# YOCO decoder trunk on one core: output pages split earlier, prev multiplications and one diagonal tile given to VectorE, group 2 scaled in one step

## The chip, the cores and the metric

The kernel runs on one core of a Trainium2 chip, in one launch. The metric is the device time of one execution in microseconds (us). TensorE is called PE, VectorE DVE, ScalarE ACT, GpSimd POOL, and SyncE, which issues the DMAs here, SP.

## What is computed

A decoder trunk over 1024 tokens of width 1024, float32, with two layers. Layer A is gated linear attention. Layer B, which the change is about, is dilated sliding-window attention with eight heads; each head attends in three groups, with window and dilation (128, 1), (512, 4) and (2048, 16), and the three results are weighted by a softmax over their log-sum-exps:

```python
for gi, (window, dilation) in enumerate(SWA_GROUPS):
    o_g, lse_g = dilated_window_attention(q[:, :, gi], k_sh[:, :, gi], v_sh[:, :, gi], window, dilation)
    outs.append(o_g); lses.append(lse_g)
wts = jax.nn.softmax(jnp.stack(lses, axis=0), axis=0)
o = jnp.sum(wts[..., None] * jnp.stack(outs, axis=0), axis=0).reshape(bsz, s, SWA_OUT)
return (o.astype(x.dtype) * jax.nn.silu(g)) @ w_out
```

Keys and values have two heads, shared by four query heads each. Behind each layer stands `layer_norm(ALPHA * x + y)`.

## The kernel before, in words

**The scheduler.** The whole kernel is written as calls on an object `S` (class `Sched`), which records them as operations. `order()` then places them one by one with a table of assumed costs: it always takes the operation that can start first by these costs and, among those, the one with the smallest priority number, which is its place in the recording; `S.later(n)` shifts that number (a negative `n` is sooner). Only then `issue()` emits all of them from one line, L446, so every row of the profile carries L446 and operations are told apart by their tiles. An operation recorded on `S.vector`, `S.scalar` or `S.gpsimd` has its engine given; `S.va` leaves the choice of DVE or ACT to the scheduler, `S.vp` that of DVE or POOL, `S.vap` that of all three. A change of any cost, engine or number of operations thus moves others too.

**Large projections.** A product with a weight matrix is made of float32r passes with both operands split into a high and a low part: `mm3` issues wh·xh, wh·xl and wl·xh, each 128x512, into a PSUM tile `acc`. `split_hi` (ACT) and `split_lo` (`S.vp`) make the parts; weights come in as `wf` and become `wh` and `wl`. Pages of 128x1024 lie in the pools `p0` and `p1` (16 each). In layer B, `p1` holds the split input x1h and x1l, `p0` the rotation tables, K, V, Q, sg and og.

**Layer B by heads.** The work runs in eight units u = 0 to 7, one for each query head. `q_proj(u)` makes Q for three groups. `scores(u)` makes score tiles `lv` and from them the exponentials P (nine tiles of 128x512) and their statistics `sts`; these go through DRAM and come back in another order as `nat`, from which DVE makes the weights `ew`; those go through DRAM again (`cwd`) and come back as `cw` (L1362 to 1405). Group 2's columns cw[16:24] need no such trip: they are copied on the chip (L1395). `attend(u)` (L1407 on) does, in this order of recording:

- multiplies each block of P by its column of `cw`, groups 2, 1, 0 (L1433 to 1437); group 2 has eight blocks of 128x64, all in one tile;
- transposes group 2's tile into one PSUM tile `ms`, copies it in four quarters (64x256) to the two block-diagonal tiles `diag` (L1446 to 1450), multiplies by V into `po` (po<-diag), and copies that to the page `og`;
- calls `turn` (L1412) twice for group 1 and twice for group 0. Each call transposes four blocks into `ms` and makes two PT tiles: `prev` is a piece of P times the identity (one or two blocks at a time, L1427), `own` is the transposed block times a triangle (`upto`, DVE), and `copy_predicated` (DVE) puts the other triangle into `prev`; the PV matmuls po<-PT follow.

`g_proj(u)` is the projection for the gate, and `close(u)` multiplies it into og and, for u < 6, writes og to DRAM as `ogB[u]`. Units 0 to 3 run `g_proj` right after their scores. For units 4 to 7 all `g_proj` are recorded after `attend(6)`, then `attend(7)` and `close(7)` (L1517 to 1522); the scheduler uses their matmuls as filling between the small steps of attention.

**The end.** All eight og pages are needed in high and low parts (ogh, ogl) for the output projection `out_ln` (columns for the first half of the tokens, banks acc, lv and po) and `out_ln_rows` (second half, with the eight weight pages woh and wol). `load_og` reads a half page of `ogB` into a staging tile `ogf` and splits it. The staging tiles share the tag "a" of 13 tiles with P, diag and the rt tiles of the layer norm. The page loads are recorded after `layer_b` (L1548 to 1555), all into `p1`, where a page comes free when the last projection has read x1h or x1l; the wo pages go into `p0` (L1564).

Of the kernel before, what the change touches and what calls it, by code (L numbers as in the profile page):

```python
# [8 lines left out]
FR = mybir.dt.float32r  # L9
# [582 lines left out]
def trunk(tc, xT, wP, wA, wA12, wAv3, w2, wO, wK, wV0, wV12, wB, wOB, par_d,  # L592
# [13 lines left out]
    def split_hi(dst, src):  # L606
        S.scalar.activation(dst, src, AF.Copy)
# [437 lines left out]
    def small(name, tag, bufs, dt=F32, shape=(128, 512)):  # L1045
        return hp.tile(list(shape), dt, name=name, tag=tag, bufs=bufs)
# [118 lines left out]
            return ap.rearrange("p (n a e) -> p n a e", n=4, a=8)  # L1165
        return ap.rearrange("p (i r) -> p i r", r=DIL[g])

    def layer_b(xs):
        bmask = hp.tile([128, 256], F32, name="bmask", bufs=1)
        S.sync.dma_start(bmask, bmask_d)  # L1170
        rmask = hp.tile([128, 64], F32, name="rmask", bufs=1)
# [130 lines left out]
        def g_proj(u):  # L1302
            sg = page(p0, F32, "sg")
            U[u]["sg"] = sg

            def evac(half, acc):
                th = small("th", "t1", 2)
                S.scalar.activation(th, acc, AF.Tanh, scale=0.5)
                S.vector.scalar_tensor_tensor(sg[:, hs(half)], th, 1.0, acc, op0=OP.add, op1=OP.mult)
            project(wB[u, 3], xs, evac)  # L1310
# [96 lines left out]
        def attend(u):  # L1407
            P, cw, Vc = U[u]["P"], U[u]["cw"], V[u // 4]
            og = page(p0, F32, "og")
            U[u]["og"] = og  # L1410

            def turn(g, j0):  # L1412

                own, prev = (small("PT", "d", 4).rearrange("p (a b) -> p a b", a=4) for _ in range(2))
                pt = ps.tile([128, 4, 128], F32, name="ms", bufs=2)
                def has(x):
                    return x.rearrange("p (a two) b -> p a two b", two=2)[:, :, 1] if g else x[:, 0 if j0 else 1:]

                with S.group():
                    for i in range(4):  # L1420
                        p, o = P[g, j0 + i]
                        S.tensor.transpose(pt[:, i, :], blk(p[:, o:], BL[g][j0 + i][2] // 128 - 1), ident)

                for i in (0, 2):
                    front = pieces(P, g, j0 + i)[0]
                    n = front.shape[1]
                    S.vp.tensor_mul(prev[:, i + 2 - n:i + 2], front, ident[:, None, :].to_broadcast([128, n, 128]))  # L1427
                S.vector.tensor_mul(own, pt, upto.to_broadcast([128, 4, 128]))
                S.vector.copy_predicated(has(prev), below.to_broadcast(list(has(prev).shape)), has(pt))
                return own, prev  # L1430


            for g in (2, 1, 0):  # L1433
                for j in range(8):
                    p, o = P[g, j]
                    x = p[:, o:o + BL[g][j][2]]
                    S.vap.scale(x, x, cw[:, column(g, j):column(g, j) + 1])

            p = P[2, 0][0]
            pt = ps.tile([128, 4, 128], F32, name="ms", bufs=2)
            with S.group():
                for i in range(4):
                    S.tensor.transpose(pt[:, i, :], blk(p, i), ident)
            for k in range(2):  # L1446
                h = slice(k * 64, k * 64 + 64)
                for s in range(2):
                    S.va.copy(diag[s][h].rearrange("p (j k q) -> p j k q", j=4, k=2)[:, :, k, :],
                              pt[h, :, s * 64:s * 64 + 64])  # L1450
            po = [ps.tile([128, 512], F32, name="po", bufs=2) for _ in range(2)]
            with S.group():
                for s in range(2):
                    for j in range(4):
                        x = s * 4 + j
                        S.tensor.matmul(po[s][:, j * 128:j * 128 + 128], blk(Vc[2], x), blk(diag[s], j),
                                         start=True, stop=True)
            for s in range(2):
                for k in range(2):
                    x = s * 8 + k * 4  # L1460
                    S.vector.tensor_copy(
                        og.rearrange("p (n a e) -> p n a e", n=8, a=8)[:, :, :, x:x + 4],
                        po[s].rearrange("p (j k a n) -> p k n a j", j=4, k=2, a=8)[:, k])
            po = [ps.tile([128, 512], F32, name="po", bufs=2) for _ in range(2)]
            started = [False, False]

            def pv(bank, outv, vblk, rhs, last=False):
                S.tensor.matmul(outv, vblk, rhs, start=not started[bank], stop=last)
                started[bank] = True


            for r0 in (0, 2):
                own, prev = turn(1, 2 * r0)
                for r in (r0, r0 + 1):
                    i = 2 * (r - r0)
                    ov = [po[i].rearrange("p (i r) -> p r i", r=4)[:, r, :] for i in range(2)]
                    pv(0, ov[0], blk(Vc[1], 2 * r), own[:, i, :])
                    pv(1, ov[1], blk(Vc[1], 2 * r), prev[:, i + 1, :])
                    pv(1, ov[1], blk(Vc[1], 2 * r + 1), own[:, i + 1, :])

            for n0 in (0, 4):
                own, prev = turn(0, n0)
                for i in range(4):
                    n = n0 + i
                    out_n = po[n // 4][:, i * 128:i * 128 + 128]
                    if n:
                        pv(n // 4, out_n, blk(Vc[0], n - 1), prev[:, i, :])
                    pv(n // 4, out_n, blk(Vc[0], n), own[:, i, :], last=(i == 3))

            for i in range(2):  # L1490
                S.vector.tensor_add(og[:, hs(i)], po[i], og[:, hs(i)])
# [13 lines left out]
        for u in range(8):  # L1505
# [9 lines left out]
            if u == 3:  # L1515
                reload_kv()
        for u in (4, 5, 6, 7):  # L1517
            g_proj(u)
            if u < 7:
                close(u)  # L1520
# [22 lines left out]

    for half in range(2):
        out_ln(0, hs(half), lambda et: load_w(wO[et]), lambda et: xT[et * 128:et * 128 + 128, :], emit_a)
    U = layer_b(x1s)

    ogs.clear()  # L1548
    for kt in range(6):
        load_og(ogB[kt], kt, p1, lambda: small("ogf", "a", 13))  # L1550
    for u in (6, 7):
        hi, lo = og_page(u, p1)
        for half in range(2):
            split_hi(hi[:, hs(half)], U[u]["og"][:, hs(half)])
            split_lo(lo[:, hs(half)], U[u]["og"][:, hs(half)], hi[:, hs(half)])

# [4 lines left out]
    wo = []  # L1561
    for kt in range(NK):
        wf = wts.tile([128, 1024], F32, name="wf", bufs=2)
        hi, lo = page(p0, FR, "woh"), page(p0, FR, "wol")  # L1564
        with S.later(-EVAC):
            S.sync.dma_start(wf.rearrange("p (e c) -> p e c", e=NK), wOB[:, :, kt, :].rearrange("e p c -> p e c"))
            split_hi(hi, wf)
            split_lo(lo, wf, hi)
        wo.append((hi, lo))
# [96 lines left out]
```

## Time and profile before

| | us |
|---|---|
| median of 3 runs | 1158.88 |
| lowest and highest run | 1158.69, 1159.53 |
| the profiled execution's own time | 1158.02 |
| its span (first to last instruction) | 1156.2 |
| what lies around the span | 1.8 |
| PE busy / DVE / ACT / POOL | 1145.3 / 816.8 / 462.4 / 187.1 |

The mean granted clock of PE in it is 0.998. A row of the timeline gives the start in us from the span's begin, the duration, engine, line, operation, output tile<-input tiles, their sizes and types, and in brackets the engine's idle time before it with the instruction that ended it. Several like instructions in a row are drawn together (x4), and then the duration is from the first start to the last end. SPq rows are DMA issues, not the transfers. A row of grouped instructions gives count, busy us, mean ns of one, and idle time before them with the releasers.

### The profile page before, as it was taken

The numbers are of one execution on the slowest core, as the hardware profiler recorded it, in microseconds if no ns is written. First come the engines' busy times: TensorE is split into PE (matmuls) and PEld (weight loads), VectorE is DVE, ScalarE is ACT, GpSimd is POOL, SyncE is SP. The second block draws the span as 40 slices with busy tenths as digits, with TensorE's granted clock in tenths as the row PEclk, the third lists the DMA queues.
The fourth block names the chain that finished last, engine by engine and source line by source line (L and its number), as shares of the span: only waits on it lengthen the run. The fifth ranks groups of instructions, "written<-read, shape, count | busy, mean of one in ns | idle before, by whom it ended". The sixth has DMA issues, their size and how long they took to land.

```text
span 1156.2 us, 19776 instructions
## 1 busy us (share of the span) xinstructions
PE 1145.3 (99%) x7780; PEld 975.7 (84%) x7780; DVE 816.8 (71%) x1653; ACT 462.4 (40%) x970; POOL 187.1 (16%) x135
## 2 busy tenths in 40 slices
PE   9999999999999999999999999999999999999997
PEld 9888888889988888888888888888888878888886
DVE  6294952695977697765366768686778788768678
ACT  5355541555473344311215342434332434435242
POOL 1001000202222121321020303030211212103000
PEclk9999999999999999999999999999999999999999
DMA  8111122111144463643611111111141111124544
GB/s 270 55 39 37 65 83 87 42 57 55 57 170 124 150 206 137 193 142 104 209 44 33 55 38 56 38 52 42 38 165 38 20 39 38 39 75 146 190 140 180
DMA packets 93374, 108.40 MB, mean 94 GB/s; under 512 B 43648, under 2 KB 61952, under 8 KB 93280
## 3 DMA queue, kind: packets, MB, share of 16 engines
q1 hardware_dynamic: 93280, 107.13, 29.5%
q8 instruction: 61, 1.00, 0.4%
q14 instruction: 33, 0.27, 0.1%
HBM read 85.94 MB, written 21.17 MB: 93 GB/s over the span
## 4 chain that ended last, share of the span: by engine, by line
PE 96%; DVE 2%; DMA 1%; ACT 0%; issue 0%; POOL 0%; DVEq 0%; SPq 0%; POOLq 0%; ACTq 0%
PE acc L446 64%; PE lv L446 9%; PE po L446 9%; PE vac L446 8%; PE ms L446 4%; PE pro L446 2%; DVE t L446 0%; DMA xf<-in_xT 0%; DVE PT L446 0%; DMA wf<-in_wB 0%; POOL wl L446 0%; DVE P L446 0%; DVE rt L446 0%; ACT P L446 0%; DVE zz L446 0%
## 5 line engine op out<-in xcount | busy, mean ns | idle before, releaser
L446 PE MATMUL acc<-x1h,wh 128*128 128x512 f32 x608 | 250.9, 413 | 0.0
L446 PE MATMUL acc<-x1h,wl 128*128 128x512 f32 x608 | 237.5, 391 | 0.0
L446 PE MATMUL acc<-x1l,wh 128*128 128x512 f32 x608 | 236.9, 390 | 0.0
L446 ACT ACTIVATE wh<-wf 128x1024 fp32r<-128x1024 f32 (+2 forms) x104 | 108.1, 1041 | 288.2 <-PE acc L446 190.5
L446 POOL TENSOR_TENSOR wl<-wf,wh 128x1024 fp32r<-128x1024 f32 x39 | 93.5, 2396 | 634.6 <-ACT wh L446 450.9
L446 PEld LDWEIGHTS acc<-x1h,wl 128*128 128x128 f32 x608 | 114.1, 188 | 24.5
L446 ACT ACTIVATE P<-P,sts 128x128 f32<-128x128 f32 (+2 forms) x192 | 81.5, 425 | 129.0 <-DVE sts L446 128.5
L446 PEld LDWEIGHTS acc<-x1l,wh 128*128 128x128 f32 x608 | 114.5, 188 | 21.1
L446 PEld LDWEIGHTS acc<-x1h,wh 128*128 128x128 f32 x608 | 114.4, 188 | 20.9
L446 DVE TENSOR_TENSOR wl<-wf,wh 128x1024 fp32r<-128x1024 f32 (+2 forms) x66 | 83.7, 1268 | 61.3 <-ACT wh L446 48.4
L446 PE MATMUL acc<-xh,wh 128*128 128x512 f32 x256 | 102.4, 400 | 0.0
L446 PE MATMUL acc<-xh,wl 128*128 128x512 f32 x256 | 99.9, 390 | 0.0
L446 PE MATMUL acc<-xl,wh 128*128 128x512 f32 x256 | 99.8, 390 | 0.0
L446 DVE TENSOR_TENSOR t<-acc,cosT 128x512 f32<-128x512 f32 x60 | 41.4, 690 | 69.4 <-PE acc L446 68.8
L446 DVE TENSOR_TENSOR t<-acc,sinT 64x512 f32<-64x512 f32 x120 | 82.6, 688 | 1.6
L446 PE MATMUL lv<-K,Q 128*64 128x64 f32 (+2 forms) x512 | 69.2, 286 | 0.0
L446 DVE CUSTOM_DVE_ANT_0 P<-lv,bmask 128x256 f32<-128x256 f32 (+1 forms) x128 | 46.9, 379 | 23.3 <-PE lv L446 22.6
L446 DVE TENSOR_TENSOR Q<-t,t 128x512 f32<-128x512 f32 x45 | 62.2, 1383 | 1.3
L446 PEld LDWEIGHTS lv<-K,Q 128*128 128x128 f32 (+1 forms) x512 | 53.8, 163 | 9.6 <-issue 1.4
L446 PE MATMUL acc<-ogh,wh 128*128 128x512 f32 x152 | 59.9, 394 | 0.0
L446 PE MATMUL acc<-ogh,wl 128*128 128x512 f32 x152 | 59.2, 389 | 0.0
L446 PE MATMUL acc<-ogl,wh 128*128 128x512 f32 x152 | 59.2, 389 | 0.0
(251 smaller groups left out, 2228.2 us busy)
## 6 DMA issues: line engine op xcount, KB each, us to landing
wf<-in_wB SPq DMA_DIRECT2D x32, 512.0 KB
wf<-in_wA SPq DMA_DIRECT2D x24, 512.0 KB
wf<-in_wO SPq DMA_DIRECT2D x16, 512.0 KB
wf<-in_wOB SPq DMA_DIRECT2D x16, 512.0 KB
wf<-in_wV SPq DMA_DIRECT2D x12, 512.0 KB
res<-in_xT SPq DMA_DIRECT2D x16, 256.0 KB
x1d<-rt SPq DMA_DIRECT2D x16, 256.0 KB
out<-rt SPq DMA_DIRECT2D x16, 256.0 KB
```

Of the source, the lines that this page charges most:

```text
L446: getattr(handle[o.eng], meth)(*[conv(a) for a in args], **{k: conv(v) for k, v in kw.items()})
```

## The change

Five edits in layer B and at its end:

- A function `early()` is called before `g_proj(7)`. It loads and splits the og pages of units 0 to 3, first half and then second half, into `p0`, with priority 1000 places sooner. Pages 4 and 5 are loaded and 6 and 7 split as before into `p1`, now also half by half.
- The wo pages of kt < 4 go into `p1`, the other four into `p0`.
- The prev multiplications of `turn` go from `S.vp` to `S.vector`: all 64 run on DVE (before, 28 did and 36 ran on POOL, 25 of them 128x128 and 11 of them 128x256).
- The eight scales of group 2 in each unit (64 in all: 38 on DVE, 23 on ACT, 3 on POOL) become one DVE multiplication of 128x512 by the broadcast columns of `cw`.
- The four diag copies have fixed engines: DVE for the first tile, ACT for the second, 16 each in all (before, ACT had 23 and DVE 9).

```diff
--- before.py
+++ after.py
@@ -1165,7 +1165,7 @@
             return ap.rearrange("p (n a e) -> p n a e", n=4, a=8)
         return ap.rearrange("p (i r) -> p i r", r=DIL[g])
 
-    def layer_b(xs):
+    def layer_b(xs, early):
         bmask = hp.tile([128, 256], F32, name="bmask", bufs=1)
         S.sync.dma_start(bmask, bmask_d)
         rmask = hp.tile([128, 64], F32, name="rmask", bufs=1)
@@ -1424,13 +1424,16 @@
                 for i in (0, 2):
                     front = pieces(P, g, j0 + i)[0]
                     n = front.shape[1]
-                    S.vp.tensor_mul(prev[:, i + 2 - n:i + 2], front, ident[:, None, :].to_broadcast([128, n, 128]))
+                    S.vector.tensor_mul(prev[:, i + 2 - n:i + 2], front, ident[:, None, :].to_broadcast([128, n, 128]))
                 S.vector.tensor_mul(own, pt, upto.to_broadcast([128, 4, 128]))
                 S.vector.copy_predicated(has(prev), below.to_broadcast(list(has(prev).shape)), has(pt))
                 return own, prev
 
 
-            for g in (2, 1, 0):
+            x = P[2, 0][0].rearrange("p (j k q) -> p k j q", j=4, k=2)
+            w = cw[:, 16:24].rearrange("p (k j one) -> p k j one", k=2, j=4)
+            S.vector.tensor_mul(x, x, w.to_broadcast([128, 2, 4, 64]))
+            for g in (1, 0):
                 for j in range(8):
                     p, o = P[g, j]
                     x = p[:, o:o + BL[g][j][2]]
@@ -1446,8 +1449,8 @@
             for k in range(2):
                 h = slice(k * 64, k * 64 + 64)
                 for s in range(2):
-                    S.va.copy(diag[s][h].rearrange("p (j k q) -> p j k q", j=4, k=2)[:, :, k, :],
-                              pt[h, :, s * 64:s * 64 + 64])
+                    (S.scalar.copy if s else S.vector.tensor_copy)(
+                        diag[s][h].rearrange("p (j k q) -> p j k q", j=4, k=2)[:, :, k, :], pt[h, :, s * 64:s * 64 + 64])
             po = [ps.tile([128, 512], F32, name="po", bufs=2) for _ in range(2)]
             with S.group():
                 for s in range(2):
@@ -1515,6 +1518,8 @@
             if u == 3:
                 reload_kv()
         for u in (4, 5, 6, 7):
+            if u == 7:
+                early()
             g_proj(u)
             if u < 7:
                 close(u)
@@ -1543,14 +1548,20 @@
 
     for half in range(2):
         out_ln(0, hs(half), lambda et: load_w(wO[et]), lambda et: xT[et * 128:et * 128 + 128, :], emit_a)
-    U = layer_b(x1s)
-
-    ogs.clear()
-    for kt in range(6):
-        load_og(ogB[kt], kt, p1, lambda: small("ogf", "a", 13))
-    for u in (6, 7):
-        hi, lo = og_page(u, p1)
+
+    def early():
+        ogs.clear()
         for half in range(2):
+            for kt in range(4):
+                with S.later(-EVAC):
+                    load_og(ogB[kt], kt, p0, lambda: small("ogf", "a", 13), (half,))
+
+    U = layer_b(x1s, early)
+    for half in range(2):
+        for kt in range(4, 6):
+            load_og(ogB[kt], kt, p1, lambda: small("ogf", "a", 13), (half,))
+        for u in (6, 7):
+            hi, lo = og_page(u, p1)
             split_hi(hi[:, hs(half)], U[u]["og"][:, hs(half)])
             split_lo(lo[:, hs(half)], U[u]["og"][:, hs(half)], hi[:, hs(half)])
 
@@ -1561,7 +1572,8 @@
     wo = []
     for kt in range(NK):
         wf = wts.tile([128, 1024], F32, name="wf", bufs=2)
-        hi, lo = page(p0, FR, "woh"), page(p0, FR, "wol")
+        q = p1 if kt < 4 else p0
+        hi, lo = page(q, FR, "woh"), page(q, FR, "wol")
         with S.later(-EVAC):
             S.sync.dma_start(wf.rearrange("p (e c) -> p e c", e=NK), wOB[:, :, kt, :].rearrange("e p c -> p e c"))
             split_hi(hi, wf)
```

The recorded operations are placed anew. PE's order is the old one up to the first `attend`, and again from the start of `out_ln`; between them the same matmuls stand in another order. Three places follow. The names: acc<-x1h, wh is a pass of a g or q projection, ms<-ident,P are transposes, po<-diag and po<-PT are attention's products with V, lv<-K,Q are scores, and acc or lv<-ogh are passes of the output projection.

On PE, around unit 4's diagonal product, the order before has:

```order
L446 MATMUL ms<-ident,P 128x128 x4
L446 MATMUL acc<-x1h_4357,wh 128x512
L446 MATMUL acc<-x1l_4368,wh 128x512
L446 MATMUL acc<-x1h_4357,wl 128x512
L446 MATMUL acc<-x1h_4379,wh 128x512
L446 MATMUL acc<-x1l_4396,wh 128x512
L446 MATMUL acc<-x1h_4379,wl 128x512
L446 MATMUL po<-diag,V_7930 128x128 x8
```

The changed kernel has there:

```order
L446 MATMUL ms<-ident,P 128x128 x4
L446 MATMUL lv<-K_7875,Q 128x128
L446 MATMUL acc<-x1h_4240,wh 128x512
L446 MATMUL acc<-x1l_4248,wh 128x512
L446 MATMUL acc<-x1h_4240,wl 128x512
L446 MATMUL acc<-x1h_4250,wh 128x512
L446 MATMUL acc<-x1l_4264,wh 128x512
L446 MATMUL acc<-x1h_4250,wl 128x512
L446 MATMUL acc<-x1h_4279,wh 128x512
L446 MATMUL acc<-x1l_4289,wh 128x512
L446 MATMUL acc<-x1h_4279,wl 128x512
L446 MATMUL po<-diag,V_7900 128x128 x8
```

Nine passes of a projection and one score block stand between the transposes and the diagonal product where six passes stood.

On PE, at unit 6's turns (V_7923 and V_7894 are group 1's values, V_7918 and V_7885 group 0's), before:

```order
L446 MATMUL po<-PT,V_7923 128x128 x12
L446 MATMUL ms<-ident,P 128x128 x8
L446 MATMUL lv<-K_7905,Q 128x256
L446 MATMUL lv<-K_7905,Q 128x128
L446 MATMUL acc<-x1h_4357,wh 128x512
L446 MATMUL acc<-x1l_4368,wh 128x512
L446 MATMUL acc<-x1h_4357,wl 128x512
L446 MATMUL po<-PT,V_7918 128x128
```

And now:

```order
L446 MATMUL po<-PT,V_7894 128x128 x6
L446 MATMUL ms<-ident,P 128x128 x4
L446 MATMUL po<-PT,V_7894 128x128 x6
L446 MATMUL po<-PT,V_7885 128x128
L446 MATMUL ms<-ident,P 128x128 x4
L446 MATMUL po<-PT,V_7885 128x128 x6
L446 MATMUL acc<-x1h_4357,wh 128x512
L446 MATMUL acc<-x1l_4368,wh 128x512
L446 MATMUL acc<-x1h_4357,wl 128x512
L446 MATMUL po<-PT,V_7885 128x128 x8
```

Group 1's twelve blocks are parted by the first transposes of group 0, and six of them, without score or projection, stand between those transposes and group 0's first block.

On PE, at unit 7's last turns, before:

```order
L446 MATMUL po<-PT,V_7923 128x128 x12
L446 MATMUL ms<-ident,P 128x128 x4
L446 MATMUL po<-PT,V_7918 128x128
L446 MATMUL acc<-ogh_9878,wh 128x512
L446 MATMUL acc<-ogl_9926,wh 128x512
L446 MATMUL acc<-ogh_9878,wl 128x512
```

And now:

```order
L446 MATMUL po<-PT,V_7894 128x128 x12
L446 MATMUL ms<-ident,P 128x128 x8
L446 MATMUL acc<-ogh_9917,wh 128x512
L446 MATMUL acc<-ogl_9930,wh 128x512
L446 MATMUL acc<-ogh_9917,wl 128x512
L446 MATMUL lv<-ogh_9917,wh 128x512
L446 MATMUL lv<-ogl_9930,wh 128x512
L446 MATMUL lv<-ogh_9917,wl 128x512
L446 MATMUL po<-PT,V_7885 128x128
```

Both groups of transposes of group 0 come first, then six passes of the output projection, and then the first block. On SP, in front of that, before:

```order
L446 DMA cwd_9735<-ew 8x8x8 x4
L446 DMA wf<-in_wOB 128x1024
L446 DMA cw<-cwd_9735 128x8x1
L446 DMA cw<-cwd_9735 128x2x4
L446 DMA ogf<-ogB_6945 128x512 x2
```

And now:

```order
L446 DMA ogf<-ogB_6390 128x512
L446 DMA ogf<-ogB_6925 128x512
L446 DMA cwd_9741<-ew 8x8x8 x2
L446 DMA ogf<-ogB_7460 128x512
L446 DMA cwd_9741<-ew 8x8x8 x2
L446 DMA ogf<-ogB_7996 128x512
L446 DMA ogf<-ogB_9520 128x512
L446 DMA cw<-cwd_9741 128x8x1
L446 DMA cw<-cwd_9741 128x2x4
```

Five half-page loads stand among the transfers of unit 7's weights, where a single weight load (wf) stood.

## The prediction

> **What bounds the kernel now.** I read the page first: the busy time of each engine, then the engines in the chain that ended last.
>
> ```profile
> PE 1145.3 (99%) x7780; PEld 975.7 (84%) x7780; DVE 816.8 (71%) x1653; ACT 462.4 (40%) x970; POOL 187.1 (16%) x135
> PE 96%; DVE 2%; DMA 1%; ACT 0%; issue 0%; POOL 0%; DVEq 0%; SPq 0%; POOLq 0%; ACTq 0%
> ```
>
> TensorE is the bound. The change leaves the number of matmuls as it is, so all that it can give is TensorE time that passes without a matmul. The table of windows says where that is: compare each stretch's length with its "PE busy".
>
> ```profile
> core 0: us, PE busy (x) PEld busy (x) DVE busy (x) ACT busy (x) POOL busy (x), PEclk, DMA share, GB/s
> 0.00:600.00 600.00, 598.63 (x4736) 509.58 (x4737) 395.79 (x572) 248.75 (x348) 89.42 (x56) 1.00 0.34 112
> 600.00:890.00 290.00, 290.00 (x1622) 247.82 (x1621) 214.00 (x567) 106.76 (x346) 56.68 (x44) 1.00 0.20 54
> 890.00:950.00 60.00, 58.88 (x365) 49.40 (x364) 49.01 (x154) 23.09 (x82) 12.38 (x11) 1.00 0.15 37
> 950.00:1050.00 100.00, 100.00 (x570) 85.94 (x569) 76.04 (x235) 44.12 (x137) 15.31 (x14) 1.00 0.21 52
> 1050.00:1062.00 12.00, 11.18 (x84) 10.31 (x83) 10.61 (x21) 5.85 (x10) 9.66 (x8) 1.00 0.83 285
> 1062.00:1148.60 86.60, 86.60 (x412) 72.68 (x410) 67.46 (x101) 33.35 (x48) 3.69 (x2) 1.00 0.48 159
> 1148.60:1156.20 7.60, 0.02 (x1) 0.00 (x0) 3.85 (x7) 0.50 (x2) 0.00 (x0) 0.75 0.35 130
> ```
>
> The 1.37 us before 600 lie in layer A and the 7.58 us at the end behind the last matmul; the change reaches neither. Between them idle are 60 - 58.88 = 1.12 us in the stretch of units 4 and 5, and 12 - 11.18 = 0.82 us at the end of unit 7: 1.94 us. The timeline of TensorE in those stretches shows each wait in its brackets.
>
> ```profile
> 898.31 1.94 PE L446 MATMUL po<-diag,V 128*128 128x128 f32 x15 [0.34 <-DVE diag L446]
> 947.06 0.70 PE L446 MATMUL ms<-ident,P 128*128 128x128 f32 x4 [0.21 <-ACT P L446]
> 948.53 0.39 PE L446 MATMUL acc<-x1l,wh 128*128 128x512 f32 x1
> 948.75 0.40 PE L446 MATMUL acc<-x1h,wl 128*128 128x512 f32 x1
> 949.72 0.46 PE L446 MATMUL po<-diag,V 128*128 128x128 f32 x2 [0.57 <-DVE diag L446]
> ```
>
> 0.34 + 0.21 + 0.57 = 1.12. A wait costs slightly more than its bracket: a 128x512 matmul follows the last after 948.75 - 948.53 = 0.22 us, yet the row at 949.72 begins 0.97 us after the one at 948.75, so 0.75 are lost where the bracket shows 0.57. I take 0.17 more for each of the four waits. The ceiling on any gain is then 1.94 + 4 x 0.17 = 2.6 us, 0.22% of the median of 1158.88 us. A measurement of this kernel tells about 0.2%, 2.3 us, from no change.
>
> **Diag copies, one engine per tile.** The four copies out of one PSUM tile stand between group 2's transposes and po<-diag. Units 4 and 5 already give one tile to DVE and the other to ACT, so the trace shows what the fixed assignment does (unit 5, DVE and then ACT):
>
> ```profile
> 947.81 0.41 DVE L446 COPY diag<-ms 64x256 f32<-64x256 f32 x1
> 949.15 0.43 DVE L446 COPY diag<-ms 64x256 f32<-64x256 f32 x1 [0.92 <-ACT diag L446]
> 948.34 0.77 ACT L446 ACTIVATE diag<-ms 64x256 f32<-64x256 f32 x2
> ```
>
> They run in series: DVE until 948.22, ACT from 948.34 to 949.11, DVE from 949.15 to 949.58. DVE's second copy waits for ACT, with which it shares nothing but the PSUM tile, and the built order of the changed kernel holds the same waits between the engines. So no pair runs side by side: 1.77 us from first start to last end, where side by side would take about 0.85. That the change doesn't do what it says is thus part of the forecast here. The Trainium skill ("PSUM — Partial Sum Buffer", section "PSUM bank collisions raise a hardware error") makes two engines on one bank and quadrant at once an error, reads against reads included, which speaks against overlap here; by a reading with overlap unit 5 would give back about 0.7 us more.
>
> In the new order unit 4 has nine acc matmuls instead of six between its transposes and po<-diag. Three more are 3 x 0.22 = 0.66 us and cover its 0.34 wait: -0.34 - 0.17 = **-0.51**. Unit 5 keeps six and the same hand-overs, DVE, ACT, ACT, DVE: its 0.57 and its 0.21 stay. In units 0 to 3 the 290 us window is full and stays so.
>
> **Group 2's weights in one step.** Removed are eight 128x64 scales a unit, mostly on DVE; added is one DVE multiplication of two 512-wide SBUF inputs. Its nearest row is that of lnA, from DVE's groups after 600.
>
> ```profile
> 946.42 0.91 DVE L446 TENSOR_SCALAR P<-P,cw 128x64 f32<-128x64 f32 x5
> L446 DVE TENSOR_TENSOR lnA<-lnA,rt 128x512 f32<-128x512 f32 x6 | 4.2, 692 | 0.2
> ```
>
> In unit 5 it takes 0.69 for the 0.91 of five scales, beside which ACT did three. That is 0.2 us earlier at the ms transposes, at most the 0.21 that the row at 947.06 waited, or 0.2 later where more engines had shared the eight. The waiting matmul's latest input may be another, so I take **0**, with -0.38 to +0.2 as ends. In the other units a full window hides it; without that cover it costs the same 0.2.
>
> **Prev multiplications from DVE or POOL to DVE.** All 64 now go to DVE; 36 leave POOL.
>
> ```profile
> L446 DVE TENSOR_TENSOR PT<-P,ident 128x256 f32<-128x256 f32 x13 | 6.5, 515 | 0.0
> L446 DVE TENSOR_TENSOR PT<-P,ident 128x128 f32<-128x128 f32 x15 | 4.4, 312 | 8.2 <-issue 6.0 <-PE po L446 2.2
> L446 POOL TENSOR_TENSOR PT<-P,ident 128x128 f32<-128x128 f32 x25 | 15.6, 644 | 11.9 <-PE po L446 6.6 <-DVE P L446 2.9 <-ACT P L446 2.4
> L446 POOL TENSOR_TENSOR PT<-P,ident 128x256 f32<-128x256 f32 x11 | 9.3, 867 | 23.5 <-PE po L446 17.2 <-DVE sts L446 6.4
> ```
>
> That adds 25 x 0.312 + 11 x 0.515 = 13.5 us to DVE, which is busy for 76.04 of 100 us in the window of units 5 to 7, so it fits; each is also 0.33 to 0.35 us shorter. It matters only where TensorE reaches PV soon after its transposes. In units 4 to 6 the new order runs "PT x6, ms x4" before the first block of group 0, so six PV blocks, twelve passes, cover DVE's work instead of eight transposes and whole turns. The end of unit 7 prices both sides:
>
> ```profile
> 1054.73 1.95 PE L446 MATMUL po<-PT,V 128*128 128x128 f32 x16
> 1056.52 0.60 PE L446 MATMUL ms<-ident,P 128*128 128x128 f32 x4
> 1057.93 0.49 PE L446 MATMUL po<-PT,V 128*128 128x128 f32 x2 [0.82 <-DVE PT L446]
> 1055.15 2.13 DVE L446 TENSOR_TENSOR PT<-P,ident 128x128 f32<-128x128 f32 x2 [0.28 <-PE po L446]
> 1057.20 0.68 DVE L446 TENSOR_TENSOR PT<-ms,upto 128x512 f32<-128x512 f32 x1
> 1057.81 0.57 DVE L446 COPY_PREDICATED PT<-below,ms 128x384 f32<-128x384 uint8 x1
> 1053.19 5.22 POOL L446 TENSOR_TENSOR ogl<-ogf,ogh 128x512 fp32r<-128x512 f32 x4
> ```
>
> Sixteen passes take 1056.52 - 1054.73 = 1.79 us, so twelve take 1.34. Against them stand 0.68 of the upto product, with 0.57 of the predicated copy partly behind the first block, and ahead of them the two prev products, 0.31 + 0.52, which can begin before the transposes end. Upto and predicated alone (1.25) just fit; with half of the prev products late, about 0.42, the excess is 0.42 + 1.25 - 1.34 = 0.33 less slack of the same order as rounding. I take 0.25 a unit for units 4 to 6: **+0.75**, between 0 (prev done early) and 0.95 a unit (0.83 late, 1.25 behind it, less 1.34, and 0.17 each), so 0 to 2.8.
>
> **Pages split during the last gates.** In the rows above the wait of 0.82 comes from a DVE product of 128x128 that took most of 2.13 us for two, where 0.312 is its mean, while POOL made four ogl splits in 5.22. In the new order six og matmuls stand between unit 7's group-0 transposes and its first block of group 0: 6 x 0.22 = 1.3 us of work that no longer waits for attention. They cover the 0.82: **-0.82 - 0.17 = -0.99**. If the pages behind those matmuls were late, this gain would be gone and a wait stand in its place.
>
> What the splits are moved past: on SP the loads of pages 0 to 3 now stand between the transfers of unit 7's softmax weights (nat, cwd, cw), and on ACT the split of a page-4 half, loaded into the staging tile that group 2's transposes free, stands ahead of scales of P.
>
> ```profile
> 1046.25 4.79 SPq L446 DMA_DIRECT2D ogf<-ogB  x5
> 1055.25 0.63 ACT L446 ACTIVATE ogh<-ogf 128x512 fp32r<-128x512 f32 x1 [0.54 <-DMA ogf<-ogB]
> 1045.27 2.79 ACT L446 ACTIVATE P<-P,cw 128x256 f32<-128x256 f32 x7
> ```
>
> A load takes 4.79 / 5 = 0.96 to issue; the last of these five, issued by 1051.04, was there at 1055.25, 4.2 later, and its split took 0.63: 5.8 us from the transposes that free the tile. Until the transposes of groups 1 and 0, TensorE has 21 og matmuls and the sixteen passes of po<-diag: 21 x 0.22 + 1.79 = 6.4. In the 0.6 that are left two scales at 2.79 / 7 = 0.40 don't quite fit. I take **+0.3** with a hand-over, between 0 (no scale behind the split) and 0.6 (three). The wo pages only change places, and from the start of out_ln TensorE's order is the old one: nothing there.
>
> **The sum.** -0.51 + 0 + 0.75 - 0.99 + 0.3 = -0.45. On the profiled execution's 1158.02 us that is 1157.57; it lies 0.86 below the median of the runs, so against that median 1158.88 - 0.45 = 1158.4. With its bounds the forecast runs from 1158.88 - 0.51 - 0.38 - 0.99 = 1157.0 to 1158.88 - 0.51 + 0.2 + 2.8 - 0.99 + 0.6 = 1161.0.
>
> **Rivals.** *All waits go.* If the copies overlap after all, or the single multiplication brings unit 5's transposes forward enough, and units 4 to 6 cost nothing, the whole ceiling comes: 1158.88 - 2.6 = 1156.3. For it speaks that DVE's latest work in unit 5 does shrink; against it the serial copies in the rows at 947.81 to 949.58.
>
> *SP's queue (slower).* A page load takes a staging tile; with P and diag holding most of the 13, two are left, so every pair of loads waits until the pair before is split, and SP issues in order: nat, cwd and cw behind a waiting load wait with it. If cw comes one load landing later than the columns cover, 4.2 - 0.6 = 3.6 us stand in front of unit 7's transposes of groups 1 and 0: 1158.4 - 0.3 + 3.6 = 1161.7. It decides once cw lands more than those 0.6 us behind the page-4 split. For it: in the old order nearly all loads came after cw (the five at 1046.25 are the first long run of them). Against it: unit 7's scores end long before, with g_proj between.
>
> *Port.* DVE operations with two SBUF inputs have been held while POOL worked:
>
> ```profile
> 944.13 1.29 POOL L446 TENSOR_TENSOR Q<-t,t 128x512 f32<-128x512 f32 x1 [4.24 <-DVE t L446]
> 944.17 1.27 DVE L446 TENSOR_TENSOR zz<-ew,sts 128x8 f32<-128x8 f32 x1
> L446 DVE TENSOR_TENSOR zz<-ew,sts x8: 153/158/1271, 636.1 to 1035.8; 128x8 f32<-128x8 f32 x8
> ```
>
> A product of 0.158 (the median) took 1.27 and ended with POOL's. All 36 moved products become open to this: 1.27 - 0.16 = 1.1 lost each time one meets a POOL split of this length. The Trainium skill ("SBUF — State Buffer", section "SBUF: two separate sides") has such a DVE instruction and GpSimd's hold the shared ports exclusively, each for its whole length; the trace agrees, 1.27 us against 0.158. POOL is busy for only 15.31 of 100 us from 950 on, so of the about six products on a tight path one or two meet it: 1158.4 + 1.6 x 1.1 = 1160.2.
>
> **How the numbers follow.** Forecast 0.60 (its time lies within 0.2%), all waits go 0.13 (faster), port 0.10 (within 0.2%), SP's queue 0.17 (slower): faster 0.13, same 0.70, slower 0.17. The range takes in the first three, with the forecast's bounds: 1156.2 to 1161.0; left out is SP's queue, 0.17.
>
> **What would show it.** Right: busy TensorE from unit 4 to the end of unit 7 but for waits of some tenths; diag copies of unit 5 still one after another with its wait of about 0.6; no 0.82 in front of the first block of group 0 in unit 7; waits of 0.2 to 0.3 for PT in units 4 to 6. Wrong: a wait of over 1 us for P, cw or ogh in unit 7, an idle stretch in units 0 to 3, DVE products of over 1 us next to POOL's ahead of a waiting PV, or no wait at all from 890 to 1062.

## The result, and the profile after

| | before | after |
|---|---|---|
| median, us | 1158.28 (22 runs, 1157.61 to 1159.53) | 1160.36 (22 runs, 1157.97 to 1162.52) |
| profiled execution, us | 1158.02 | 1160.66 |
| its span, us | 1156.2 | 1158.9 |

The ratio after to before is 1.0017, with a 95% interval of 1.0011 to 1.0023. The changed kernel is slower by about 2 us, where 0.45 us faster was forecast. The time lies inside the range, and the change is smaller than the 0.2% named there, but its sign is the other one, and with 22 runs of each that is clear of the noise. The runs also spread over 4.6 us where those of before spread over 1.9.

First the busy times and the windows of the changed kernel, cut as before; the last matmul now starts 3.1 us later, so the end of the sixth window has moved.

```profile
PE 1146.7 (99%) x7780; PEld 976.2 (84%) x7780; DVE 821.7 (71%) x1662; ACT 452.0 (39%) x935; POOL 174.1 (15%) x105
core 0: us, PE busy (x) PEld busy (x) DVE busy (x) ACT busy (x) POOL busy (x), PEclk, DMA share, GB/s
...
600.00:890.00 290.00, 290.00 (x1621) 247.80 (x1620) 215.50 (x586) 101.82 (x326) 48.10 (x24) 1.00 0.20 54
890.00:950.00 60.00, 58.95 (x370) 49.88 (x369) 50.16 (x155) 19.88 (x74) 10.62 (x7) 1.00 0.16 37
950.00:1050.00 100.00, 99.53 (x563) 85.29 (x562) 75.08 (x216) 40.96 (x124) 12.38 (x9) 1.00 0.23 62
1050.00:1062.00 12.00, 11.91 (x73) 10.15 (x72) 11.26 (x26) 8.70 (x20) 4.47 (x3) 1.00 0.68 199
1062.00:1150.00 88.00, 85.92 (x416) 71.50 (x415) 68.59 (x101) 31.42 (x44) 9.23 (x7) 1.00 0.48 156
```

POOL is less busy (174.1 for 187.1 us) and DVE a little more, as the moved products say. TensorE's idle time has moved: 0.47 us from 950 to 1050, where there was none, and 2.08 us from 1062 to 1150, where there was none. Its timeline names the waits:

```profile
946.57 0.63 PE L446 MATMUL ms<-ident,P 128*128 128x128 f32 x4 [0.57 <-DVE sts L446]
...
949.05 1.13 PE L446 MATMUL po<-diag,V 128*128 128x128 f32 x8 [0.49 <-DVE diag L446]
...
997.91 2.02 PE L446 MATMUL po<-diag,V 128*128 128x128 f32 x16 [0.47 <-DVE diag L446]
...
1065.76 0.50 PE L446 MATMUL acc<-ogl,wh 128*128 128x512 f32 x1 [1.80 <-DVE ogl L446]
...
1128.46 0.50 PE L446 MATMUL ms<-sum,onesr 128*128 128x512 f32 x1 [0.23 <-DVE sum L446]
```

The waits of 0.34 (unit 4) and 0.82 (unit 7) are gone, but a new one of 1.80 us stands at the first low part of the og matmuls put in to cover the 0.82. What the other engines do ahead of it, first DVE, then POOL, then ACT:

```profile
1061.39 2.64 DVE L446 TENSOR_TENSOR PT<-P,ident 128x128 f32<-128x128 f32 x2
1063.95 2.35 DVE L446 TENSOR_TENSOR ogl<-ogf,ogh 128x512 fp32r<-128x512 f32 x2
```

```profile
1061.20 1.27 POOL L446 TENSOR_TENSOR ogl<-og,ogh 128x512 fp32r<-128x512 f32 x1 [5.86 <-ACT ogh L446]
1062.42 1.32 POOL L446 TENSOR_TENSOR ogl<-ogf,ogh 128x512 fp32r<-128x512 f32 x1
1063.71 1.44 POOL L446 TENSOR_TENSOR ogl<-og,ogh 128x512 fp32r<-128x512 f32 x1
```

```profile
1059.33 1.27 ACT L446 ACTIVATE ogh<-ogf 128x512 fp32r<-128x512 f32 x2 [2.68 <-DMA ogf<-ogB]
```

The high parts were there by 1060.6, so the load was not what came last. DVE's low parts stood behind two prev products that took 2.64 us. (A row that draws like instructions together gives the shape of the first; the second is 128x256, and the means are 0.312 and 0.515.) Then the low parts took 2.35 themselves. Nearly all of this, 1061.39 to 1066.30, lies beside three POOL splits in a row from 1061.20 to 1065.15. This is the forecast's rival "Port", but not at the products that it named: these two ran on DVE before the change as well (the 2.13 us row at 1055.15). The second theme is unit 6: DVE's second copy comes last of the four there, and TensorE waits for it.

```profile
996.08 0.42 DVE L446 COPY diag<-ms 64x256 f32<-64x256 f32 x1 [0.39 <-PE ms L446]
997.33 0.43 DVE L446 COPY diag<-ms 64x256 f32<-64x256 f32 x1 [0.83 <-ACT diag L446]
```

### The profile page after: what moved, and what is told of

It reads as the page before. It is cut to its first block, busy times and chain, and to the rows that moved or that the text cites. A ratio compares the mean times of both kernels' runs of the same rounds, so it can differ in the third digit from the quotient of the medians.

```text
span 1158.9 us, 19708 instructions
## 1 busy us (share of the span) xinstructions
PE 1146.7 (99%) x7780; PEld 976.2 (84%) x7780; DVE 821.7 (71%) x1662; ACT 452.0 (39%) x935; POOL 174.1 (15%) x105
## 4 chain that ended last, share of the span: by engine, by line
PE 92%; DVE 4%; DMA 2%; issue 1%; ACT 1%; DVEq 0%; ACTq 0%
PE acc L446 63%; PE po L446 8%; PE lv L446 8%; PE vac L446 8%; PE ms L446 4%; PE pro L446 2%; DMA wf<-in_wOB 2%; DVE rt L446 1%; DVE wol L446 0%; DVE PT L446 0%; ACT woh L446 0%; DVE t L446 0%; DVE P L446 0%; DVE ogl L446 0%; DVE sq L446 0%
## 5 line engine op out<-in xcount | busy, mean ns | idle before, releaser
L446 DVE TENSOR_TENSOR Q<-t,t 128x512 f32<-128x512 f32 x41 | 56.9, 1389 | 1.3
```

Of the source, the lines that this page charges most:

```text
L446: getattr(handle[o.eng], meth)(*[conv(a) for a in args], **{k: conv(v) for k, v in kw.items()})
```

## The experiments

Two theories came out of this. **Port**: in unit 7, DVE's operations on two SBUF tiles are held while POOL's splits run. **Order of the copies**: in units 5 and 6 the tile that po<-diag needs first is finished last. Rivals: the pages simply land late; the sum of four serial copies counts, not their order; DVE is overloaded; another edit is at fault. Five of the experiments keep a kernel's placed order, taken from `order()`, and alter only the operations named; the others undo a part and let the scheduler place anew. Each was timed beside the kernel before, which took 1158.49 us for the first eight and 1158.52 for the last two (1158.28 beside the changed kernel).

**1. The three splits on VectorE.** In the changed kernel's order:

```diff
-        done = self.order()
+        done = _placed(self.order())
+    last = [o for o in done if o.eng == "POOL" and o.writes and o.writes[0].buf.name[:3] == "ogl"]
+    for o in last[-5:-2]:
+        o.eng = "DVE"
```

> The changed kernel in its own order of instructions, but the three low-part splits that GpSimd makes at the end of unit 7 (two halves of page 6, one of page 5) are made by VectorE at their place in the order. Port theory: VectorE's two-input operations were held while GpSimd worked (2.64 us for two products, 2.35 for two splits), so the wait of 1.80 us for ogl goes, with about 0.18 of refill: 2.0 us less than the changed kernel, about 1158.4, and the spread of the runs shrinks. Rival, late pages: the loads land late whoever splits them, the wait stays and VectorE has 2 us more to do: no less than the changed kernel's 1160.4, up to 2 more. Rival, VectorE overloaded at that place: slower than the changed kernel.

Measured: 1158.49 us (1157.80 to 1160.06), 1.9 less than the changed kernel; ratio to before 1.0002 (0.9993 to 1.0011). DVE's operations at the same place:

```profile
1061.28 0.63 DVE L446 TENSOR_TENSOR PT<-P,ident 128x128 f32<-128x128 f32 x2
1061.83 1.29 DVE L446 TENSOR_TENSOR ogl<-ogf,ogh 128x512 fp32r<-128x512 f32 x2
```

0.63 and 1.29 us instead of 2.64 and 2.35, though DVE has three splits more to do, and the wait for ogl is gone. The pages were not late, and DVE was not overloaded. The profiled execution is the slowest of the eleven (1160.06): it waits 0.76 us in two places for weight pages of the output projection (wol), of which more below.

**2. Both copies of the first tile first.** In the changed kernel's order:

```diff
+    at = [i for i, o in enumerate(done) if o.calls[0][0] in ("copy", "tensor_copy") and o.writes[0].buf.name == "diag"]
+    for u in range(0, len(at), 4):
+        four = sorted((done[i] for i in at[u:u + 4]), key=lambda o: o.seq)
+        if u // 4 in (5, 6):
+            for i, k in zip(at[u:u + 4], (0, 2, 1, 3)):
+                done[i] = four[k]
```

> The changed kernel in its own order, but in units 5 and 6 both copies of the first diagonal tile (VectorE) come ahead of both of the second (ScalarE); the engines stay. Theory: the fixed engines finish the tile that TensorE needs first as the last of the four copies, and that makes the waits of 0.49 (unit 5) and 0.47 us (unit 6) before the diagonal product; both go, with 0.17 us of refill each: 1.3 us less, about 1159.1. Rival, it is the sum of four serial copies that counts, not their order: the waits move to the second tile's four blocks, and 0.4 us or less is gained. Rival, the gain is lost again at the end behind the late pages: the profile shows no wait in units 5 and 6, and the time stays at 1160.4.

Measured: 1159.47 us (1157.39 to 1161.44), 0.9 less than the changed kernel, which is not clear of the noise with runs that spread so far; ratio to before 1.0005 (0.9996 to 1.0014). The trace is clear. In unit 6, DVE, ACT and TensorE with this order:

```profile
995.10 0.86 DVE L446 COPY diag<-ms 64x256 f32<-64x256 f32 x2 [0.40 <-PE ms L446]
996.05 0.77 ACT L446 ACTIVATE diag<-ms 64x256 f32<-64x256 f32 x2 [0.91 <-DVE diag L446]
996.05 0.40 PE L446 MATMUL acc<-x1h,wl 128*128 128x512 f32 x1
996.29 1.39 PE L446 MATMUL po<-diag,V 128*128 128x128 f32 x11
```

No wait for diag in either unit, with four copies as serial as before: it is their order. Unit 7's po<-diag comes at 1051.70 instead of 1053.34, 1.64 earlier; 0.25 of that was there already at unit 5's transposes (946.32 for 946.57). Its wait for ogl, still 1.22 us, stays, and the profiled execution also waits 0.76 us for a weight page of the output projection, so not all of it arrives.

**3. Both together.** 

> The changed kernel's order with both mendings: the three low-part splits at the end of unit 7 on VectorE, and in units 5 and 6 both copies of the first diagonal tile first. If the two causes are separate, their gains add: 1160.4 - 1.9 - 1.3 = 1157.2, faster than before by about 1 us. If a load that lands late stands behind both (the pages of unit 7, or the weights of the output projection), what the copies give is lost there again: about 1158.5.

Measured: 1157.27 us (1156.90 to 1158.66); ratio to before 0.9990 (0.9981 to 1.0000). The gains add, as two separate causes would. The view of waits has two lines left, the first of them in layer A:

```profile
PE pro L446 <- DVE Dg L446: 1.2, 1, 1.2
PE ms L446 <- DVE sts L446: 0.6, 1, 0.6
```

**4. Splits on VectorE, and the same work put back on GpSimd for nobody.** On top of experiment 1; the mask tile bmask that it overwrites is no longer read at that point:

```diff
+    mask = next(v for o in done for v in o.reads if v.buf.name == "bmask").buf
+    again = View(mask, _np.broadcast_to(_np.arange(256).reshape(1, 256), (128, 256)))
+    for o in last[-5:-2]:
+        for half in (slice(0, 256), slice(256, 512)):
+            c = Op()
+            c.eng, c.func, c.first = "POOL", None, []
+            c.calls = [(m, (again, a[1][:, half], a[2][:, half]), kw) for m, a, kw in o.calls]
+            done.insert(done.index(o), c)
```

> The mended splits of unit 7 (three splits on VectorE) with three splits' work put back on GpSimd at the same place: it subtracts the same tiles in two halves each into the mask tile, which nobody reads any more, so nothing waits for it. Only GpSimd's presence beside VectorE differs. Port theory: VectorE's products and splits beside it are held again, products of 1 us and over in the trace, TensorE waits about 2 us for ogl or PT, 1160.4 or more. Rival, GpSimd's split was late as a producer and contention counts for nothing: the time stays at 1158.5 and the products at their 0.3 us.

Measured: 1159.76 us (1158.88 to 1160.87), 1.3 more than experiment 1; ratio to before 1.0013 (1.0004 to 1.0022). DVE and POOL at the place:

```profile
1061.12 0.84 DVE L446 TENSOR_TENSOR PT<-P,ident 128x128 f32<-128x128 f32 x2
1061.88 2.35 DVE L446 TENSOR_TENSOR ogl<-ogf,ogh 128x512 fp32r<-128x512 f32 x2
1064.15 0.68 DVE L446 TENSOR_TENSOR PT<-ms,upto 128x512 f32<-128x512 f32 x1
```

```profile
1060.74 1.81 POOL L446 TENSOR_TENSOR bmask<-og,ogh 128x256 f32<-128x256 f32 x2 [5.67 <-ACT ogh L446]
1062.63 2.21 POOL L446 TENSOR_TENSOR bmask<-ogf,ogh 128x256 f32<-128x256 f32 x2
```

Nothing waits for these POOL operations, and the two splits are back at 2.35 from 1.29. That shows contention without any dependence, and it costs TensorE a wait that experiment 1 does not have:

```profile
1069.06 1.16 PE L446 MATMUL po<-PT,V 128*128 128x128 f32 x8 [0.77 <-DVE PT L446]
```

The wait and the time are less than expected (about 2 us, 1160.4 or more): the two products ahead of the splits took 0.84, not far from the 0.63 of experiment 1, so less was held than in the changed kernel. It is the mechanism of the prediction's rival "Port". The Trainium skill ("SBUF — State Buffer", section "SBUF: two separate sides") puts it as an exclusive lock held for the whole instruction. The trace agrees: 1.06 us more for two splits, about one POOL operation of the row above (2.21 us for two).

**5. The early pages alone.** The kernel before with `early()` and the places of the wo pages, nothing else. Seen from the changed kernel, in extract:

```diff
-                    S.vector.tensor_mul(prev[:, i + 2 - n:i + 2], front, ...)
+                    S.vp.tensor_mul(prev[:, i + 2 - n:i + 2], front, ...)
...
-            S.vector.tensor_mul(x, x, w.to_broadcast([128, 2, 4, 64]))
-            for g in (1, 0):
+            for g in (2, 1, 0):
...
-                    (S.scalar.copy if s else S.vector.tensor_copy)(
+                    S.va.copy(
```

> The kernel before with only the early page splits (and the places of the wo pages); prev products, scales and diagonal copies are chosen by the scheduler as before. If the loss lies in the early pages at the end of unit 7: slower than before by 1 us or more, a wait for ogh or ogl in unit 7. If it lies in the edits of attend, or in the two together: the same as before or up to 1 us faster, since the wait of 0.82 us in unit 7 may go.

Measured: 1158.47 us (1157.44 to 1159.90); ratio to before 1.0001 (0.9992 to 1.0009). The early pages alone cost nothing and bring nothing that the runs tell; unit 7's wait for PT is 0.72 instead of 0.82.

**6. The edits of attend alone.** The changed kernel with the page loads, `p0` and `p1` of before, in extract:

```diff
-    U = layer_b(x1s, early)
+    U = layer_b(x1s)
...
-            if u == 7:
-                early()
```

> The changed kernel without the early splits: prev products on VectorE, one multiplication for group 2, and fixed engines for the diagonal copies. If the loss lies in the early pages: within 0.6 us of before (unit 4's 0.51 gained, up to 0.9 lost by the order of the copies in units 5 and 6), about 1158.5. If it lies in attend: slower than before by 1 us or more.

Measured: 1166.38 us (1165.87 to 1167.14); ratio to before 1.0067 (1.0054 to 1.0081). The loss was expected here if it lay in attend (1 us or more), but not of this size. Unit 7's weights come late: cw is issued at 1046.45 where before issued it at 1040.80 (SP's rows; before first).

```profile
1040.80 1.00 SPq L446 DMA_DIRECT2D cw<-cwd  x2
```

```profile
1046.45 1.00 SPq L446 DMA_DIRECT2D cw<-cwd  x2
```

The scales and the prev products then fall on POOL's splits. TensorE, DVE (for the scales the tile's view, with shortest, median and longest in ns), and POOL:

```profile
1060.74 1.22 PE L446 MATMUL po<-PT,V 128*128 128x128 f32 x4 [3.54 <-DVE PT L446]
```

```profile
L446 DVE TENSOR_SCALAR P<-P,cw x8: 340/850/1462, 1050.8 to 1056.9; 128x256 f32<-128x256 f32 x7, 128x128 f32<-128x128 f32 x1
```

```profile
1057.20 1.41 DVE L446 COPY og<-po 128x256 f32<-128x256 f32 x4
1058.53 1.55 DVE L446 TENSOR_TENSOR PT<-P,ident 128x128 f32<-128x128 f32 x2
1060.00 0.68 DVE L446 TENSOR_TENSOR PT<-ms,upto 128x512 f32<-128x512 f32 x1
1060.60 0.43 DVE L446 COPY_PREDICATED PT<-below,ms 128x256 f32<-128x256 uint8 x1
```

```profile
1049.83 2.37 POOL L446 TENSOR_TENSOR wl<-wf,wh 128x1024 fp32r<-128x1024 f32 x1 [3.84 <-ACT wh L446]
1052.46 2.54 POOL L446 TENSOR_TENSOR ogl<-ogf,ogh 128x512 fp32r<-128x512 f32 x2 [0.26 <-ACT ogh L446]
1055.58 1.29 POOL L446 TENSOR_TENSOR ogl<-ogf,ogh 128x512 fp32r<-128x512 f32 x1 [0.57 <-ACT ogh L446]
1058.56 5.22 POOL L446 TENSOR_TENSOR ogl<-ogf,ogh 128x512 fp32r<-128x512 f32 x4 [1.70 <-ACT ogh L446]
```

A scale takes 0.34 us at its shortest and up to 1.46 here. Unit 7's waits are 0.24, 0.36, 0.84 and 3.54 us, 4.2 more than the 0.82 of before. Of the rest of the 8, the most is TensorE's clock: from the long wait on it was granted at half for some microseconds (windows as above; the clock is the third number from the end).

```profile
1060.00:1062.00 2.00, 1.26 (x5) 1.27 (x6) 2.00 (x5) 0.84 (x2) 2.00 (x2) 0.50 0.68 219
1062.00:1066.00 4.00, 4.00 (x17) 3.71 (x17) 2.23 (x5) 2.49 (x5) 2.74 (x3) 0.50 0.25 88
1066.00:1068.00 2.00, 2.00 (x16) 1.87 (x15) 1.25 (x3) 0.00 (x0) 0.39 (x1) 0.96 0.00 0
```

From 1060.74 to 1066 half of 5.3 us is lost, some 2.6 us by estimate. In the changed kernel cw is issued later still, yet no scale is waited for; 21 og matmuls of the early pages now stand on TensorE between group 2's transposes and those of groups 1 and 0:

```profile
1050.53 1.00 SPq L446 DMA_DIRECT2D cw<-cwd  x2
```

So with attend edited as it is, the early pages save 6 us. What moved DVE's weight chain back was not tried apart.

**7. The kernel before, with both copies of the first tile first, in units 4 and 5.** The edit of experiment 2 with `(4, 5)`, in the order of before.

> The kernel before in its own order, but in units 4 and 5 both copies of the first diagonal tile come ahead of both of the second, engines as they are. If it is the order of the copies that makes TensorE wait, the 0.34 of unit 4 and the 0.57 of unit 5 go, with 0.17 of refill each: 1.25 us less than before, about 1157.2. If the four serial copies count as a whole: the same as before.

Measured: 1157.07 us (1156.70 to 1159.24); ratio to before 0.9991 (0.9982 to 1.0000), 1.4 us less in the medians. In unit 5, DVE, ACT and TensorE:

```profile
947.68 0.85 DVE L446 COPY diag<-ms 64x256 f32<-64x256 f32 x2
```

```profile
948.63 0.77 ACT L446 ACTIVATE diag<-ms 64x256 f32<-64x256 f32 x2 [0.42 <-DVE diag L446]
```

```profile
948.86 1.39 PE L446 MATMUL po<-diag,V 128*128 128x128 f32 x11
```

The first tile is ready at 948.53; TensorE starts at 948.86 without a wait, while ACT still copies the second. This is, with experiment 3, the fastest kernel of the study.

**8. Without the prev edit.** The first hunk of experiment 5's diff, in the changed kernel.

> The changed kernel with the prev products left to the scheduler's choice of VectorE or GpSimd, as before. If moving them to VectorE is what lays the tight products beside GpSimd's splits, the 1.8 us wait in unit 7 goes and the time is about 1158.5. If the wait belongs to the early pages and their splits alone, it stays: about 1160.4. GpSimd's products of 0.64 to 0.87 us on the path of PT may cost up to 1 us by themselves.

Measured: 1158.08 us (1156.34 to 1159.59); ratio to before 0.9998 (0.9989 to 1.0007). The wait for ogl is gone. The products beside POOL's splits are still slow:

```profile
1058.40 2.33 DVE L446 TENSOR_TENSOR PT<-P,ident 128x128 f32<-128x128 f32 x2 [0.55 <-PE po L446]
```

But in this order no split that TensorE needs next is queued behind them. Unit 6's wait for diag is gone as well: its copies now run DVE, ACT, DVE, ACT, and the first tile is finished by the third. So of the edits this one, on top of the others, decides whether these two waits stand, by the order that follows from it and not by the products' own time.

**9 and 10. Without the fixed engines; without the one multiplication.** The third and the second hunk of experiment 5's diff, each by itself in the changed kernel.

> The changed kernel with the diagonal copies' engines left to the scheduler. It still puts units 5 and 6 in the order VectorE first tile, ScalarE, ScalarE, VectorE first tile, and the end of unit 7 is the changed kernel's but for the copies. If the fixed engines are not the cause of either wait, both stay (0.5 us in units 5 and 6, 1.8 in unit 7): about 1160.4. If they are: about 1159.1 or less.

Measured: 1160.00 us (1158.92 to 1161.61); ratio to before 1.0013 (1.0004 to 1.0022). The waits of 0.48 and 0.47 in units 5 and 6 are unchanged; in unit 7, 0.90 for ogl and 0.87 for PT make the same sum as the 1.80. The fixed engines are not the cause: left free, the scheduler puts the copies of units 5 and 6 in the same order.

> The changed kernel with eight scales of group 2 in place of the one multiplication. The end of unit 7 has the same order on TensorE and GpSimd as the changed kernel, so by the port theory the wait for ogl stays there, near 1.8 us. In units 5 and 6 the second copy of the first diagonal tile now comes third of four instead of last: its waits should shrink by about 0.4 us each. Together 1159.6. If the one multiplication is what makes unit 7 late, the wait for ogl goes and the time is 1158 or less.

Measured: 1160.25 us (1158.83 to 1162.38); ratio to before 1.0016 (1.0007 to 1.0025). The wait for ogl is there with 1.78 us, as the port theory has it. The waits for diag did not shrink as expected: 0.40, 0.39 and 0.49 in units 4, 5 and 6. I had misread that order: only unit 5 has the first tile's second copy third, and its wait is 0.39 instead of 0.49; units 4 and 6 have it last. Unit 4 has six passes again ahead of its diagonal product, so its wait is back, and unit 5 has its three passes again ahead of its transposes, whose wait of 0.57 is gone.

## Why the prediction was wrong

Counted from the brackets of the two profiled executions, with the prediction's 0.17 for each wait that comes or goes (an estimate):

| step | forecast | measured |
|---|---|---|
| unit 4's po<-diag | -0.51 | -0.51 |
| unit 5's po<-diag | 0 | -0.08 |
| unit 5's transposes | 0 (-0.38 to +0.2) | +0.36 |
| unit 6's po<-diag | not in the sum | +0.64 |
| PT in units 4 to 6 | +0.75 | 0 |
| unit 7: the 0.82 before PT | -0.99 | -0.99, and +0.26 at group 1's first block |
| unit 7: pages ahead of their matmuls | +0.3 | +1.97 |
| output projection | 0 | +0.40 |
| sum | -0.45 | +2.05 |

The two profiled executions differ by 2.64 us. Of the 0.6 left over, 0.4 was there before anything changed on TensorE: unit 0's first transposes start at 653.17 instead of 652.78, and up to there its order is the old one. The last matmul starts 3.08 us later (1151.42 for 1148.34), so another 0.6 behind that point is not traced; the part after the last matmul is 0.4 shorter.

**The step that failed**, the largest of several, is "Pages split during the last gates": that the six og matmuls were "work that no longer waits for attention". They do not wait for attention's data, but their low parts are made on DVE, in DVE's queue behind attention's prev products, and beside POOL. The sentence "if the pages behind those matmuls were late, this gain would be gone and a wait stand in its place" is what happened, only that no load was late: experiments 1 and 4 show that POOL's neighbouring splits made DVE late, 1.97 us where the sum had +0.3. The sign that I had listed as wrong, DVE products of over 1 us next to POOL's, is in the trace. The rival "Port" had the mechanism and nearly the time (1160.2), with a chance of 0.10. The time is in part luck: it priced moved products, while the held ones had been on DVE before; it lacked the 0.64 and 0.36 of units 6 and 5, and it had a +0.75 that did not come. I had seen the hold in the very row that I used for the gain (2.13 us for two products beside 5.22 us of POOL; I read both as 128x128, but the second, of 128x256, took 1.50) and credited its removal without asking where POOL's next splits would fall.

**Diag copies.** That they stay serial held in every trace. (The two halves lie on different partitions, 0 to 63 and 64 to 127, so the rule on bank and quadrant that the prediction leaned on bears on two copies of the same half alone. Why the others are serial as well was not tested.) But I priced only their sum. Unit 5 was taken as evidence that the hand-overs do not change, and unit 6 was not looked at: before, its first tile was finished by the third copy, on ACT at 997.25, and TensorE came just then; now it is finished by the last. Before, ACT and TensorE:

```profile
996.87 0.38 ACT L446 ACTIVATE diag<-ms 64x256 f32<-64x256 f32 x1 [0.48 <-DVE diag L446]
997.31 0.94 PE L446 MATMUL po<-diag,V 128*128 128x128 f32 x6
```

Experiments 2 and 7 show the order at work, in both kernels.

**PT in units 4 to 6.** The +0.75 was not there: no wait for PT before unit 7. That is the end of the range that I gave as 0, with the prev products done early.

**Unit 5's transposes** wait 0.36 longer because TensorE is there sooner: in the new order three passes fewer stand between the scores and the transposes. That group 2's multiplication itself, 0.69 us, is no loss was right.

**Unit 4** came out as worked out. **SP's queue** did not decide: cw came 10 us later, and the matmuls of the early pages covered it; the 0.09 at group 1's first block is all that can be left of the +0.3.

**Output projection.** The waits of 0.2 to 0.8 us for sum and wol appear in the changed kernel and in experiments 1, 2, 4, 7 and 8, and not in 3, 5, 6, 9 and 10 or in the profile before. Experiment 7, which loads its pages as before, has one of 0.22. The weight pages follow one another through two buffers. ACT's idle time for their loads from 1070 on differs between the profiled executions, but the waits do not follow it: 16.8 us before, 17.7 in the changed kernel, 23.4 in experiment 2, and 22.1 in experiment 3, where TensorE never waited. Whether the change adds to it stays open.

## What to carry to other kernels

Before crediting a gain to work that is moved beside a tight spot, look at which engine makes its operands and what runs beside that engine there: here a VectorE operation on SBUF tiles next to a GpSimd one took up to its own time plus most of a GpSimd operation's (a scale of 0.34 us took 1.41 beside a split of 1.27). Where several serial steps feed one consumer, finish first what the consumer takes first; reordering two copies took away waits of 0.34 to 0.57 us a unit here, without a new instruction, and was worth 1.2 us in experiment 3 over experiment 1 and 1.4 in experiment 7. When a scheduler places the work anew, no single edit has a price of its own: the edits of attend cost 8 us alone, 2 us with the early pages, and the early pages alone nothing.

## What the runs showed of the hardware

- Not every DVE operation is held. In experiment 6, while POOL ran four splits from 1058.56 to 1063.78, the products of P and ident took 1.55 us for two (0.48 in the changed kernel at 1058.57, with POOL idle), but the product with a PSUM operand (PT<-ms,upto) kept its 0.68 and copy_predicated its 0.43.
- Scales of one SBUF tile by a column are held too: 0.34 us with POOL idle, 1.36 to 1.46 beside POOL's splits (experiment 6).
- The granted clock can fall behind a long wait of TensorE. In experiment 6 it was 0.50 for some 5 us behind 3.54 us. Behind nearly the same wait for ogl it fell in the profiled execution of experiment 10 (1.78 us) and not in that of the changed kernel (1.80). The two kernels, experiment 10 first:

```profile
1066.00:1071.00 5.00, 5.00 (x23) 4.37 (x23) 3.31 (x7) 0.00 (x0) 0.00 (x0) 0.66 0.00 0
1066.00:1071.00 5.00, 5.00 (x34) 4.40 (x34) 4.66 (x9) 0.03 (x1) 0.00 (x0) 1.00 0.00 0
```

  It may be a part of why the changed kernel's runs spread: its longest execution, 1162.52 us, has a mean clock of 0.996, the other 21 have 0.998 or 0.999. That the wait brings the fall about was not tested, and most of the spread is not explained (4.6 us over 22 runs, 4.1 in experiment 2 and 3.6 in 10, but 2.7 in 9, which has the same splits beside DVE, and 2.0 in 4).
